# One encoder layer on one core: the mixer's shift and scale in four quarters, each followed by its k/v and q matmuls, and the third group's state update issued behind the gated norm

## The chip, the core and the metric

The kernel runs on one core of a Trainium2 chip. The metric is the device time of one execution in microseconds (us); lower is better. Five engines with queues of their own share the work: TensorE (PE) multiplies, VectorE (DVE), ScalarE (ACT) and GpSimd (POOL) work on tiles in SBUF and PSUM, and SyncE (SP) issues the DMA transfers. Each queue is carried out in order.

## The reference

One layer (DEPTH = 1) of a streaming encoder, for a prompt of 1024 rows and for eight samples of 16 rows, all with model width 1024:

```python
mod = (silu(c) @ w_ada + b_ada)                    # c: one row for the prompt, eight for the samples
sh1, sc1, g1, sh2, sc2, g2 = split(mod, 6)         # each 1024 wide
h = rms_norm(x, norm_mix) * (1 + sc1) + sh1
proj = h @ w_in                                    # z, x/B/C, dt of the SSD heads; q; k and v
y_ssd = ssd_mixer(proj[..., :D_SSD_IN], ...)       # conv, scan in chunks of 64, state update, gated norm
q = rms_norm(q, q_norm); k = rms_norm(k, k_norm)
o = banded_sink_attention(q, k, v, ...)            # window 128, sinks, ALiBi
x = x + g1 * (concat([y_ssd, o]) @ w_out)
h = rms_norm(x, norm_ffn) * (1 + sc2) + sh2
x = x + g2 * ((silu(gate) * up) @ w_down)          # up and gate after a causal conv of width 3
```

The gated norm of the SSD heads is `y = rms_norm(y * silu(z), norm_g)`. The scan also returns its last state, for the prompt and for each of the eight samples.

## The kernel before

**Tiling.** The 1152 rows are three groups g = 0, 1, 2 of 384; the samples are the last 128 rows of g = 2. Activations lie with features on the partitions, in eight feature tiles kt = 0 to 7 of 128. Each fp32 product is three matmuls (`mm3`, L290 to L292): both operands are split in a high part (`wh`, `Rh`) and the rest (`wl`, `Rl`), and high by high, high by low and low by high are added up in PSUM.

**Weights.** `unit` (L74 to L89) loads a unit of 512 KB in one of five buffers `raw` (SP), makes `wh` with a cast on ACT (L80), and `wl` with a subtraction (L86): of q units on POOL, of the others on DVE. There are three buffers of each. For g = 0 each `wl` of the units `kv`, `q`, `f` and `o` is also written to a DRAM tensor `low_*`, and g = 1 and g = 2 read it from there. `W(key)` makes units in the order of `plan` up to two ahead.

**Shift and scale.** The chunks of `w_ada` (512 KB each) pass through the same five `raw` buffers; a chunk is four small matmuls (L156). `ada(c)` adds up eight chunks, copies the sum to `ms` (L174), transposes it (L162) and adds the bias, which gives `mod` (L166); `scale_rows` makes A1 = norm_mix times (1 + sc1) from it (L191). For the mixer this comes in two halves, `ada_half(0)` and `ada_half(1)`, each for four feature tiles of both shift and scale. `mod_steps` then makes, for each feature tile, the scaled row (L251, DVE), the high part `Rh` with the shift (L252, ACT) and the low part `Rl` (L253, DVE). For g = 0 the rows lie in the two tiles `z` (kt 0 to 3) and `qT` (kt 4 to 7).

**The mixer, group by group.** `kv_mm` multiplies k, v and dt (units kv 0 and 1, four feature tiles each), `q_mm` q (units q 0 to 3, two feature tiles each), and `s1_f` the other columns of the projection (ten units f, PSUM tiles named s_f). For g = 0 units kv 0, q 0 and q 1 are multiplied behind the first half and kv 1, q 2 and q 3 behind the second. `attention(g)`, `modulate(g + 1)` and `s1_f(g)` follow. `ssd(g)` is written at the start of the turn of g + 1: for each of three row tiles t, `ssd_1` (decays, masked products; L633 to L666), `ssd_2` (outputs and state; L686 to L723) and `ssd_3` (the gated norm: a sum L752, `rstdy` on DVE L754 and POOL L755, a matmul that spreads it over the partitions L757, then L759 to L761). For g = 2 `ssd_state` (L726 to L743) updates the samples' states: eight multiplies L740 and four adds L742 on tiles of 64x512 and 128x512, and a load and a store each. It is written behind `ssd_3` of the last tile. `out_proj` and then the gated MLP (L987, and `acc` at L1234 to L1240) take the rest.

**What sets the order.** A scheduler places the instructions of all engines by simulated times when the kernel is built; what is ready early in its simulation is placed early, wherever it is written. `tc.issue_after(x)` (used by the change) holds the instructions of a block behind instruction x in that order. On the chip each queue then runs in the order that was laid down.

## Time and profile before

| | us |
|---|---|
| median of three runs | 1321.71 |
| the three runs | 1320.98, 1321.71, 1325.16 |
| the profiled execution, whole time | 1326.11 |
| its span in the trace | 1324.3 |
| granted TensorE clock, mean over the span | 0.976 |

The profile is of one execution, which took 4.4 us longer than the median and 1.8 us longer than its own span. In the rows a line number is a line of the kernel before; `out<-in` names tiles. Starts are microseconds from the start of the span. A bracket at the end of a row is the time for which the engine had been idle, and what released it.

### The profile page before, as it was taken

To read this page: it belongs to the slowest core of one execution; us is meant where nothing else is said; L and a number is where in the kernel's file an instruction comes from. 1 tells how busy PE (TensorE), PEld (TensorE's weight loads), DVE (VectorE), ACT (ScalarE), POOL (GpSimd) and SP (SyncE) were. 2 spreads that over 40 slices of the span, in tenths; PEclk is the share of its full clock that TensorE was granted. 3 is DMA by queue.
4 is the path that set the end of the run, shared out by engine and by line. 5 is a ranking of instruction groups with operands and counts; after the bars stand their busy time and mean duration, and the time that the engine had idled before them with its cause. 6 is when DMAs were issued, how large, how long until landed. Compare 5 with 4: busy or idle time off the path is not lost.

```text
span 1324.3 us, 22453 instructions
## 1 busy us (share of the span) xinstructions
PE 1269.5 (96%) x8545; PEld 1191.4 (90%) x8545; DVE 901.2 (68%) x1793; ACT 626.0 (47%) x1077; POOL 195.6 (15%) x242
## 2 busy tenths in 40 slices
PE   3899989999999899979999999999999999999998
PEld 1688768888878799979999999999999999999998
DVE  4387798566884864796877887766676755654653
ACT  3267736664566425554544445454545433333331
POOL 1131244344310420000011111000000000000000
PEclk8899989999999989989999999999999999999999
DMA  9886524785668469422434434323232897787751
GB/s 346 291 311 214 194 96 173 258 313 218 226 251 287 145 215 358 156 95 85 146 121 139 155 112 130 119 85 121 86 120 73 287 390 239 262 266 221 252 186 51
DMA packets 99948, 257.93 MB, mean 195 GB/s; under 512 B 16544, under 2 KB 47904, under 8 KB 99456
## 3 DMA queue, kind: packets, MB, share of 16 engines
q1 hardware_dynamic: 99840, 256.49, 55.9%
q8 instruction: 67, 1.10, 0.3%
q14 instruction: 41, 0.34, 0.1%
HBM read 202.06 MB, written 54.39 MB: 194 GB/s over the span
## 4 chain that ended last, share of the span: by engine, by line
PE 86%; DVE 9%; DMA 1%; issue 1%; ACT 1%; SPq 0%; POOL 0%; DVEq 0%; ACTq 0%
PE P L987 34%; PE acc L292 7%; PE acc L291 7%; PE acc L290 7%; PE s_f L290 3%; PE s_f L292 3%; PE s_f L291 3%; PE out_proj L290 2%; PE out_proj L292 2%; PE out_proj L291 2%; PE attn_o L532 2%; PE ada L156 2%; PE attn_t L519 1%; PE s_q L292 1%; PE s_q L291 1%
## 5 line engine op out<-in xcount | busy, mean ns | idle before, releaser
L987 PE MATMUL P<-T,wh 128*128 128x288 f32 x704 | 206.5, 296 | 8.2 <-ACT T L915 5.5
L987 PE MATMUL P<-T,wl 128*128 128x288 f32 x704 | 208.1, 296 | 0.0
L80 ACT CAST wh<-raw 128x1024 fp32r<-128x1024 f32 (+1 forms) x138 | 144.8, 1050 | 79.4 <-PE out_proj L292 22.5
L291 PE MATMUL acc<-gh,wl 128*128 128x384 f32 x520 | 174.5, 337 | 0.0
L292 PE MATMUL acc<-gl,wh 128*128 128x384 f32 x520 | 173.0, 337 | 0.3 <-DVE gl L1235 0.3
L290 PE MATMUL acc<-gh,wh 128*128 128x384 f32 x520 | 172.2, 337 | 0.0
L987 PEld LDWEIGHTS P<-T,wh 128*128 128x128 f32 x704 | 132.6, 189 | 8.9 <-ACT T L915 5.7
L987 PEld LDWEIGHTS P<-T,wl 128*128 128x128 f32 x704 | 133.2, 189 | 0.0
L1094 DVE SCALAR_TENSOR_TENSOR uy<-uraw,fw,uy 128x1024 f32<-128x1024 f32 x88 | 112.5, 1279 | 22.6 <-ACT uy L1091 22.5
L86 DVE TENSOR_TENSOR wl<-raw,wh 128x1024 fp32r<-128x1024 f32 (+1 forms) x86 | 107.4, 1248 | 29.2 <-ACT wh L80 29.1
L972 DVE TENSOR_TENSOR wl<-raw,wh 128x512 fp32r<-128x512 f32 x132 | 87.1, 685 | 49.5 <-ACT wh L971 49.5
L1234 ACT CAST gh<-gu 128x384 fp32r<-128x384 f32 x65 | 33.3, 513 | 156.4 <-PE acc L291 142.2
L292 PEld LDWEIGHTS acc<-gl,wh 128*128 128x128 f32 x520 | 98.0, 189 | 0.6 <-DVE gl L1235 0.6
L291 PEld LDWEIGHTS acc<-gh,wl 128*128 128x128 f32 x520 | 97.6, 188 | 0.1
L290 PEld LDWEIGHTS acc<-gh,wh 128*128 128x128 f32 x520 | 97.5, 188 | 0.0
L971 ACT CAST wh<-raw 128x512 fp32r<-128x512 f32 x132 | 76.4, 620 | 31.6 <-PE P L987 30.5
L290 PE MATMUL s_f<-Rh,wh 128*128 128x384 f32 x240 | 83.2, 347 | 0.0
L292 PE MATMUL s_f<-Rl,wh 128*128 128x384 f32 x240 | 82.1, 342 | 0.0
L291 PE MATMUL s_f<-Rh,wl 128*128 128x384 f32 x240 | 81.8, 341 | 0.0
L1124 ACT COPY tm<-P 128x576 f32<-128x576 f32 x48 | 30.5, 635 | 106.5 <-PE P L987 95.2
L1233 DVE TENSOR_TENSOR gu<-gu,gg 128x384 f32<-128x384 f32 x65 | 35.8, 556 | 64.6 <-DMA gu<-gd 51.7
L1096 POOL COPY fso<-uraw 128x2 f32<-128x2 f32 x44 | 11.1, 252 | 447.9 <-DVE uraw L1079 447.9
(357 smaller groups left out, 3424.2 us busy)
## 6 DMA issues: line engine op xcount, KB each, us to landing
raw<-in_w_down SPq DMA_DIRECT2D x66, 512.0 KB, 4.3
raw<-in_w_up SPq DMA_DIRECT2D x50, 512.0 KB, 3.8
gd<-uy SPq DMA_DIRECT2D x44, 576.0 KB, 3.2
raw<-in_w_ada SPq DMA_DIRECT2D x48, 512.0 KB, 6.1
raw<-in_w_f SPq DMA_DIRECT2D x30, 512.0 KB, 5.6
gu<-gd SPq DMA_DIRECT2D x65, 192.0 KB, 3.7
gg<-gd SPq DMA_DIRECT2D x65, 192.0 KB, 3.7
raw<-in_w_out SPq DMA_DIRECT2D x24, 512.0 KB, 4.9
```

Source lines behind the costliest of these rows:

```text
L80: S.copy(wh[:, :n], raw[:, :n])
L86: eng.tensor_tensor(wl[:, :n], raw[:, :n], wh[:, :n].bitcast(F32), op=ALU.subtract)
L290: T.matmul(ps, lh, rh, start=first, stop=False)
L291: T.matmul(ps, ll, rh, start=False, stop=False)
L292: T.matmul(ps, lh, rl, start=False, stop=last)
L971: S.copy(h, x)
L972: V.tensor_tensor(l, x, h.bitcast(F32), op=ALU.subtract)
L987: T.matmul(ps[:, c, 0:HC], x[:, m], y[:, kt, cc], start=first and kt + n == 0, stop=kt == 3 and n == 2, skip_group_check=True)
L1094: V.scalar_tensor_tensor(y[:, :1024], raw[:, j:j + 1024], k[:, j:j + 1], y[:, :1024], op0=ALU.mult, op1=ALU.add)
L1124: S.copy(two(dst), bk(ps))
L1233: V.tensor_tensor(gu, gu, gg, op=ALU.mult)
L1234: S.copy(gh, gu)
```

## The change

The shift and scale of the mixer are made by `ada_quarter(j)` for j = 0 to 3, four chunks of 512 KB each, laid out anew (`w_ad0`) so that a quarter holds shift and scale of feature tiles 2j and 2j + 1; the sum over the model width is now made of two half-sums, added on DVE. Behind each quarter come two feature tiles of `mod_steps`, half a kv unit (18 matmuls) and one q unit (18 matmuls). All k, v and q matmuls of g = 0 are thus written ahead of `s1_kv`.

In `unit`, the low parts of kv and q of g = 0 are made on DVE and not written to DRAM. At g = 1 they are made again, q on POOL and kv on DVE, and written then; g = 2 reads them as before.

For g = 1 each load of a tile `xs` in `mod_steps` is preceded by a copy of one column of A1 into that tile, so that it can't start ahead of the last quarter.

`ssd_state` of g = 2 is put in an `issue_after` block behind the last instruction of `ssd_3`.

```diff
@@ unit
         nm, g, u = k
-        if nm in lows and g > 0:
+        keep = 1 if nm in ("kv", "q") else 0
+        if nm in lows and g > keep:
             nc.sync.dma_start(out=wl[:, :n].bitcast(F32), in_=lows[nm][u])
             return wh, wl
-        eng = G_ if nm in sys_wp else V
+        eng = G_ if nm in sys_wp and g > 0 else V
         eng.tensor_tensor(wl[:, :n], raw[:, :n], wh[:, :n].bitcast(F32), op=ALU.subtract)
-        if nm in lows:
+        if nm in lows and g == keep:
             nc.sync.dma_start(out=lows[nm][u], in_=wl[:, :n].bitcast(F32))
@@ in place of ada
+    def ada_quarter(j):
+        ps = (cps, mps)[j % 2]("ada")
+        for kp in range(4):
+            raw = rawt()
+            nc.sync.dma_start(out=raw[:, :1024], in_=d["w_ad0"][j, kp])
+            for i in range(4):
+                g = 32 * i
+                T.matmul(ps[g:g + 32, :256], cs[:, 2 * kp + i // 2, :], raw[:, i * 256:(i + 1) * 256],
+                         start=kp == 0, stop=kp == 3, tile_position=(0, g))
         ms = ft([P, 256], "ms", 1)
         V.tensor_copy(ms, ps[:, :256])
-        ada_end(c, ms, ps)
+        p2 = ps[:, 256:]
+        for i in range(2):
+            T.transpose(p2[:, i * P:(i + 1) * P], ms[:, i * P:(i + 1) * P], ident)
...
+        V.tensor_tensor(m, v[:, 0:2], b.unsqueeze(3).broadcast_to([P, 2, 2, 9]), op=ALU.add)
+        V.tensor_tensor(m, m, v[:, 2:4], op=ALU.add)
+        f = slice(2 * j, 2 * j + 2)
+        V.scalar_tensor_tensor(A1[:, f, :], mod[:, 8 + 2 * j:10 + 2 * j, :], 1.0,
+                               C["nm"][:, f].unsqueeze(2).broadcast_to([P, 2, 9]), op0=ALU.add, op1=ALU.mult)
@@ mod_steps
                 xs = ft([P, GN], "xs", 3)
+                if g == 1:
+                    V.tensor_copy(xs[:, 0:1], A1[:, 7, 0:1])
                 nc.sync.dma_start(out=xs, in_=src[:, kt, :])
@@ kv_mm
-    def kv_mm(g, h, ps, us, ws=None):
+    def kv_mm(g, h, ps, us, ws=None, ks=range(4)):
@@ ssd
         if g == 2:
-            ssd_state(one[2] + (hBs,))
+            with tc.issue_after(traced()):
+                ssd_state(one[2] + (hBs,))
@@ the start
-    ada_half(0)
-    ws = [W(k, 0) for k in (("kv", 0, 0), ("q", 0, 0), ("q", 0, 1))]
+    ada_quarter(0)
...
+    for j in range(4):
+        if j % 2 == 0:
+            kvw = W(("kv", 0, j // 2), 0)
+        qw = W(("q", 0, j), 0)
+        for _ in range(2):
+            next(steps, None)
+        if j < 3:
+            ada_quarter(j + 1)
+        kv_mm(0, h, kvps, [j // 2], kvw, (2 * (j % 2), 2 * (j % 2) + 1))
+        q_mm(0, h, qps, [j], qw)
```

On SyncE, the loads at the start of the kernel. Before, behind `cs`, `xT` and `cst`:

```order
L153 DMA raw<-in_w_ada 128x1024 x5
L237 DMA xs<-in_xT 128x384 x3
L153 DMA raw<-in_w_ada 128x1024 x3
L77 DMA raw<-in_w_kv 128x1056
L77 DMA raw<-in_w_q 128x1024 x2
L153 DMA raw<-in_w_ada 128x1024 x2
L88 DMA low_kv<-wl 128x1056
L153 DMA raw<-in_w_ada 128x1024
L88 DMA low_q<-wl 128x1024
L153 DMA raw<-in_w_ada 128x1024 x2
L88 DMA low_q<-wl 128x1024
L153 DMA raw<-in_w_ada 128x1024 x3
```

After, behind the same loads:

```order
L174 DMA raw<-in_w_ad 128x1024 x4
L77 DMA raw<-in_w_kv 128x1056
L77 DMA raw<-in_w_q 128x1024
L174 DMA raw<-in_w_ad 128x1024 x4
L77 DMA raw<-in_w_q 128x1024
L174 DMA raw<-in_w_ad 128x1024 x4
L77 DMA raw<-in_w_kv 128x1056
L77 DMA raw<-in_w_q 128x1024
L174 DMA raw<-in_w_ad 128x1024 x4
L77 DMA raw<-in_w_q 128x1024
L291 DMA raw<-in_xk 128x1024 x3
L77 DMA raw<-in_w_f 128x1024 x4
```

The weights of k, v and q now stand between the quarters' chunks, the writes of `low_kv` and `low_q` are gone from here, and the first loads of `xs` and of the units f stand behind all of it.

On VectorE, `ssd(0)` at its gated norm of the first row tile, while the weights of g = 1 are made. Before (`rstdy` is the norm's factor, `wl` a weight's low part, `sz` the state):

```order
L715 TENSOR_TENSOR sz<-sz,ssd_st 64x256 x2
L86 TENSOR_TENSOR wl<-raw,wh 128x1024
L754 TENSOR_SCALAR rstdy<-ssd_n 128x1
L750 TENSOR_REDUCE ys<-qn 128x128
L759 SCALAR_TENSOR_TENSOR z<-z,cst,ssd_n 128x128 x4
```

After:

```order
L733 TENSOR_TENSOR sz<-sz,ssd_st 64x256 x2
L772 TENSOR_SCALAR rstdy<-ssd_n 128x1
L87 TENSOR_TENSOR wl<-raw,wh 128x1024
L768 TENSOR_REDUCE ys<-qn 128x128
L777 SCALAR_TENSOR_TENSOR z<-z,cst,ssd_n 128x128 x4
```

The factor `rstdy` (L754 before, L772 after) has passed one making of a low part.

On VectorE, `ssd(2)` from the sum of the first row tile's norm to its factor. Before (`qT` holds the samples' states, `P` their decays):

```order
L750 TENSOR_REDUCE ys<-qn 128x128
L652 TENSOR_SCALAR PT<-ssd_rp,acs 128x128 x4
L740 TENSOR_TENSOR qT<-qT,P 64x512 x4
L714 TENSOR_TENSOR sz<-sz,P 64x256
L656 TENSOR_TENSOR PT<-PT,GT 128x512
L665 TENSOR_TENSOR xdt<-ssd_px,dt 128x512
L714 TENSOR_TENSOR sz<-sz,P 64x256
L719 SCALAR_TENSOR_TENSOR xbc<-xbc,cst,ssd_y 128x128 x4
L740 TENSOR_TENSOR qT<-qT,P 64x512 x2
L656 TENSOR_TENSOR PT<-PT,GT 128x512
L715 TENSOR_TENSOR sz<-sz,ssd_st 64x256
L754 TENSOR_SCALAR rstdy<-ssd_n 128x1
```

After, from the same sum:

```order
L768 TENSOR_REDUCE ys<-qn 128x128
L670 TENSOR_SCALAR PT<-ssd_rp,acs 128x128 x4
L732 TENSOR_TENSOR sz<-sz,P 64x256
L674 TENSOR_TENSOR PT<-PT,GT 128x512
L683 TENSOR_TENSOR xdt<-ssd_px,dt 128x512
L732 TENSOR_TENSOR sz<-sz,P 64x256
L737 SCALAR_TENSOR_TENSOR xbc<-xbc,cst,ssd_y 128x128 x4
L674 TENSOR_TENSOR PT<-PT,GT 128x512
L733 TENSOR_TENSOR sz<-sz,ssd_st 64x256 x2
L772 TENSOR_SCALAR rstdy<-ssd_n 128x1
```

The six state multiplies (L740 before, L758 after) are gone from ahead of `rstdy`; they now stand behind the last instruction of the third tile's gated norm (L779), and one small instruction on `sz` has come ahead of `rstdy`.

## Rows read from the trace of the kernel before

**Rows 1.** The page: busy time of PE; its busy tenths in 40 slices.

```profile
PE 1269.5 (96%) x8545; PEld 1191.4 (90%) x8545; DVE 901.2 (68%) x1793; ACT 626.0 (47%) x1077; POOL 195.6 (15%) x242
...
PE   3899989999999899979999999999999999999998
```

**Rows 2.** Three stretches: length, busy us of each engine, clock, DMA share, GB/s.

```profile
20.00:40.00 20.00, 12.77 (x79) 7.63 (x80) 10.41 (x13) 5.74 (x8) 4.65 (x2) 0.66 0.96 362
...
180.00:200.00 20.00, 14.60 (x74) 12.22 (x73) 17.63 (x38) 6.60 (x11) 6.15 (x6) 0.66 0.30 105
...
460.00:480.00 20.00, 16.36 (x82) 15.80 (x83) 17.28 (x34) 3.91 (x7) 7.46 (x7) 0.66 0.63 218
```

**Rows 3.** PE in time, the start: start, duration, line, operation, [idle before].

```profile
14.27 5.35 PE L156 MATMUL ada<-raw,cs 128*32 128x256 f32 x48 [0.30 <-issue]
...
22.90 1.08 PE L156 MATMUL ada<-raw,cs 128*32 128x256 f32 x8 [1.49 <-DMA raw<-in_w_ada]
...
32.34 1.03 PE L290 MATMUL s_kv<-wh,Rh 128*128 128x264 f32 x3 [3.24 <-ACT Rh L252]
...
54.63 0.62 PE L290 MATMUL s_kv<-wh,Rh 128*128 128x264 f32 x3 [1.92 <-ACT Rh L252]
...
72.50 0.59 PE L290 MATMUL s_f<-Rh,wh 128*128 128x384 f32 x2
```

**Rows 4.** PE in time, pairs of successive matmuls at the start of the kernel.

```profile
46.00 0.39 PE L291 MATMUL s_q<-wh,Rl 128*128 128x512 f32 x1
46.23 0.40 PE L292 MATMUL s_q<-wl,Rh 128*128 128x512 f32 x1
...
61.40 0.63 PE L290 MATMUL s_q<-wh,Rh 128*128 128x512 f32 x1
61.83 0.63 PE L291 MATMUL s_q<-wh,Rl 128*128 128x512 f32 x1
...
64.13 0.28 PE L292 MATMUL s_kv<-wl,Rh 128*128 128x264 f32 x1
64.25 0.29 PE L290 MATMUL s_kv<-wh,Rh 128*128 128x264 f32 x1
```

**Rows 5.** DVE in time, the two scale steps of the start.

```profile
26.63 2.35 DVE L191 SCALAR_TENSOR_TENSOR A<-mod,cst 128x36 f32<-128x36 f32 x1
29.09 4.14 DVE L251 SCALAR_TENSOR_TENSOR z<-z,A,rs 128x384 f32<-128x384 f32 x4
...
53.08 0.20 DVE L191 SCALAR_TENSOR_TENSOR A<-mod,cst 128x36 f32<-128x36 f32 x1
```

**Rows 6.** POOL in time, two low parts of q weights.

```profile
26.57 4.65 POOL L86 TENSOR_TENSOR wl<-raw,wh 128x1024 fp32r<-128x1024 f32 x2 [11.47 <-ACT wh L80]
```

**Rows 7.** DVE in time, `ssd(0)` ahead of the first gated norm.

```profile
184.58 1.61 DVE L86 TENSOR_TENSOR wl<-raw,wh 128x1024 fp32r<-128x1024 f32 x1
```

**Rows 8.** PE's waits: line waited for, us in total, times, longest.

```profile
PE ssd_n L757 <- POOL rstdy L755: 10.0, 3, 5.5
```

**Rows 9.** DVE in time, `ssd(2)`: the state multiplies and the factor.

```profile
453.54 2.77 DVE L740 TENSOR_TENSOR qT<-qT,P 64x512 f32<-64x512 f32 x4
...
459.49 2.35 DVE L740 TENSOR_TENSOR qT<-qT,P 64x512 f32<-64x512 f32 x2
...
462.81 0.14 DVE L754 TENSOR_SCALAR rstdy<-ssd_n 128x1 f32<-128x1 f32 x1
```

**Rows 10.** PE in time, the same stretch and the matmuls behind it.

```profile
457.24 0.28 PE L752 MATMUL ssd_n<-cst,ys 128*128 128x1 f32 x2
...
463.64 0.79 PE L757 MATMUL ssd_n<-cst,rstdy 128*128 128x128 f32 x2 [5.49 <-POOL rstdy L755]
...
476.25 0.48 PE L292 MATMUL out_proj<-Rl,wh 128*128 128x384 f32 x1
476.57 0.34 PE L290 MATMUL out_proj<-Rh,wh 128*128 128x384 f32 x1
476.75 0.34 PE L291 MATMUL out_proj<-Rh,wl 128*128 128x384 f32 x1
```

More of the change, by code (lines that the diff above doesn't have):

```diff
@@ L152, in ada_mm @@
             raw = rawt()
-            nc.sync.dma_start(out=raw[:, :1024], in_=d["w_ada"][c, kt])
+            nc.sync.dma_start(out=raw[:, :1024], in_=d["w_ada"][c - 2, kt])
             for i in range(4):
@@ L163, in ada_end @@
         v = p2.rearrange("p (i g r) -> p g i r", i=2, g=4)[:, :, :, 0:9]
-        for f0, a, b in ((4 * c, 0, 2), (8 + 4 * c, 2, 4)) if c < 2 else ((8 * c, 0, 4),):
-            f1 = f0 + 2 * (b - a)
-            V.tensor_tensor(mod[:, f0:f1, :].rearrange("p (g i) r -> p g i r", i=2), v[:, a:b],
-                            C["bada"][:, f0:f1].rearrange("p (g i) -> p g i", i=2).unsqueeze(3)
-                            .broadcast_to([P, b - a, 2, 9]), op=ALU.add)
-    def ada(c, bank):
-        ps = bank("ada")
-        ada_mm(ps, c, 0, 8)
+        f0 = 8 * c
+        V.tensor_tensor(mod[:, f0:f0 + 8, :].rearrange("p (g i) r -> p g i r", i=2), v,
+                        C["bada"][:, f0:f0 + 8].rearrange("p (g i) -> p g i", i=2).unsqueeze(3)
+                        .broadcast_to([P, 4, 2, 9]), op=ALU.add)
+    def ada_quarter(j):
[7 more added lines that the diff above has]
+                         start=kp == 0, stop=kp == 3, tile_position=(0, g))
         ms = ft([P, 256], "ms", 1)
         V.tensor_copy(ms, ps[:, :256])
-        ada_end(c, ms, ps)
+        p2 = ps[:, 256:]
+        for i in range(2):
+            T.transpose(p2[:, i * P:(i + 1) * P], ms[:, i * P:(i + 1) * P], ident)
+        v = p2.rearrange("p (i g r) -> p g i r", i=2, g=4)[:, :, :, 0:9]
+        m = mod[:, 0:16, :].rearrange("p (s j i) r -> p s j i r", s=2, j=4)[:, :, j]
+        b = C["bada"][:, 0:16].rearrange("p (s j i) -> p s j i", s=2, j=4)[:, :, j]
+        V.tensor_tensor(m, v[:, 0:2], b.unsqueeze(3).broadcast_to([P, 2, 2, 9]), op=ALU.add)
[3 more added lines that the diff above has]
+                               C["nm"][:, f].unsqueeze(2).broadcast_to([P, 2, 9]), op0=ALU.add, op1=ALU.mult)
     def ada_part(i):
@@ L315, in kv_mm @@
             for t in range(3):
-                for k in range(4):
+                for k in ks:
                     kt = 4 * u + k
@@ L806, in out_proj @@
         rstd_of(ss, 1024, rstd2[:, g, :])
-    def ada_half(half):
-        ada(half, (mps, cps)[half])
-        scale_rows(A1, C["nm"], 2, half)
     x0 = [ft([P, 4, GN], tag) for tag in ("z", "qT")]
@@ L821, in body @@
     r = s0_stats(0, x0)
-    ada_half(0)
-    ws = [W(k, 0) for k in (("kv", 0, 0), ("q", 0, 0), ("q", 0, 1))]
+    ada_quarter(0)
     h = [R(), R()]
     kvps = [gps("s1_kv") for _ in range(3)]
+    qps = [cps("s1_q") for _ in range(3)]
     steps = mod_steps(0, x0, r, A1, 0, h)
-    for kt in steps:
-        if kt == 3:
-            break
     next(steps)
-    ada_half(1)
-    qps = [cps("s1_q") for _ in range(3)]
-    kv_mm(0, h, kvps, [0], ws[0])
-    q_mm(0, h, qps, [0], ws[1])
-    q_mm(0, h, qps, [1], ws[2])
-    for kt in steps:
-        pass
+    for j in range(4):
[8 more added lines that the diff above has]
+        q_mm(0, h, qps, [j], qw)
     hs = {0: h}
@@ L859, in body @@
             mixS[g - 1] = ssd(g - 1, *dat[g - 1])
[L860 to L862 removed]
+        if g > 0:
             kvps = [gps("s1_kv") for _ in range(3)]
@@ L1295 @@
     A["cT"] = cT
-    wa = I["w_ada"][0].reshape(8, P, 12, 512)[:, :, [0, 2, 1, 3] + list(range(4, 12))]
-    A["w_ada"] = cc(wa.reshape(8, P, 6, 1024).transpose(2, 0, 1, 3))
+    wa = I["w_ada"][0]
+    A["w_ad0"] = cc(wa[:, :2048].reshape(4, 2, P, 2, 4, 256).transpose(4, 0, 2, 1, 3, 5).reshape(4, 4, P, 1024))
+    A["w_ada"] = cc(wa[:, 2048:].reshape(8, P, 4, 1024).transpose(2, 0, 1, 3))
     wi = I["w_in"][0]
```

7 lines of the change are left out of this document (1 added, 6 removed).

## The prediction

> **What bounds the kernel now.** I read first the page: TensorE is busy for 1269.5 of 1324.3 us, and of the 40 slices of the span only a few hold less than nine tenths [rows 1]. So a change can win only where TensorE stands still or runs at the lower of its two clocks (2.4 and 1.2 GHz). Next I read the stretches, to find where that is: 20 to 40 us has 12.77 busy of 20 at a mean granted clock of 0.66, 180 to 200 us 14.60 at 0.66, 460 to 480 us 16.36 at 0.66 [rows 2]. The change touches all three, so each was read in TensorE's order of time.
>
> In the start the reader is to see waits for an ada sum and what is made from it: 1.49 us for a chunk, 3.24 us until the first k/v matmul at 32.34, and 1.92 us behind the second half at 54.63; the first matmul of s_f comes at 72.50 [rows 3]. The three slices behind it, 66 to 165 us, show nines [rows 1], so an earlier 72.50 should move what follows with it. In `ssd(0)` and `ssd(2)` TensorE waits for the factor of the gated norm, 10.0 us in three waits, the longest 5.5 [rows 8].
>
> **Part 1, the quarters.** *What a quarter costs.* Successive q matmuls start 0.23 us apart at the full clock and 0.43 at the low one; k/v matmuls 0.12 at the full clock [rows 4]; at the low one I take twice that, 0.24 or a little less. A quarter has 18 of each: 18 x 0.12 + 18 x 0.23 = 6.3 us at the full clock, about 11.8 at the low one. Four ada chunks cost 4 x 1.08 = 4.3 at the low clock [rows 3] and, halved, 2.2 at the full one; two transposes, by the k/v matmuls the nearest in width, stay under 0.5. That is 9.0 us a quarter, and with about 0.4 for handing on the rows 9.4. Its loads are four chunks, a q unit and half a kv unit, 2.9 MB; at the 362 GB/s of 20 to 40 us [rows 2] 8.0 us, just under TensorE's 9.4.
>
> *When the first begins.* Six chunks are done 5.35 us after 14.27 [rows 3], so four by about 17.9. In the old start the end of the eight chunks (22.90 + 1.08 = 23.98) and the first k/v matmul lie 8.4 us apart. Of this the step for A took 2.35 us where the same step took 0.20 in the second half, and the four steps on z 4.14 [rows 5], while POOL was making low parts of q, 4.65 us from 26.57 [rows 6]. The change puts these on VectorE, at most 1.61 us each by the one seen there [rows 7]; A comes in quarters of the size, with an add more (about 0.2, the duration of the unhindered A). I take 3.6 us in place of 8.4 and get 17.9 + 3.6 = 21.5.
>
> The Trainium skill, "SBUF — State Buffer", section "SBUF: two separate sides", says that VectorE with two inputs in SBUF and a GpSimd instruction that reads SBUF share a port pair as an exclusive lock, and the later one waits in full. The long A and the long first step on z agree with it; by that rule the start gains and `ssd(0)`, below, pays.
>
> *The sum of the start.* The first quarter runs in part at the low clock, and its q unit waits for one of five raw buffers: 13.0 us to the start of the second (9.4, some 2.5 for five us at half the rate, 1.1 for the load). The third begins 9.3 later, the fourth 9.0 later, and its own matmuls, with a cast of an f unit ahead of its `Rh` on ACT, take 6.6: 21.5 + 13.0 + 9.3 + 9.0 + 6.6 = 59.4. Against 72.5 this is **13 us gained**; 8 if each quarter waits some 1.7 us more (as behind the second half, 1.92 [rows 3]), 15 if the first warms up sooner.
>
> *Taken at nothing.* The six writes of low parts leave the start and come back at g = 1 in place of six loads of the same size, under full TensorE work and little DMA (105 GB/s in 180 to 200 us [rows 2]). Eight copies of a column cost some 0.16 us each on VectorE, by the smallest of the rows, 0.14 [rows 9]: 1.3 us, under the matmuls of s_f; without that cover it would be 1.3 on the path.
>
> **Part 2, ssd(0).** The low parts of q are now made on POOL at g = 1, four of 4.65 / 2 = 2.3 us [rows 6], between the products of `ssd(0)`. Where VectorE runs an instruction with two tiles beside one, it may stretch up to that length: from 0 to 4 x 2.4 = 9.6 us, in a stretch where it is near its limit (17.63 of 20 [rows 2]). On the other side `rstdy` stood behind a low part of 1.61 us [rows 7], now ahead of it, and four more q matmuls (0.9 us) stand where TensorE waited. I take a **gain of 2**, bounds a loss of 9 and a gain of 5: two of the four stand on POOL ahead of the work that VectorE hurries with, and the two kv low parts that VectorE gets come early.
>
> **Part 3, ssd(2).** The sum of the first tile's norm is ready at 457.5, but the factor comes on VectorE only at 462.81, behind six state multiplies of 2.77 and 2.35 us [rows 9]; TensorE stands still for 5.49 us and then runs at the low clock up to 476.25: out_proj matmuls come 0.32 us apart there and 0.17 to 0.18 behind it [rows 10]. With the six gone (5.12) and one state add put ahead (half the columns of a multiply of 2.77 / 4, some 0.4), the factor comes some 4.4 us earlier, and TensorE's wait shrinks to about 1.1. If the clock stays up after so short a wait, the 12.6 us from 463.64 to 476.25 take half, 6.3 less. That is 10.7; I take **10** since the first tile's outputs behind the factor must also be ready sooner than they had to be. The bounds: 4.4 if the clock falls all the same, 12 if the other two norms gain as well.
>
> *What is queued behind.* The six multiplies and three adds now stand behind the last gated norm in one row, about 7 us of VectorE; behind them wait the evictions of out_proj. Three PSUM banks of 24 matmuls (24 x 0.175 = 4.2 us each) cover 8.4, so I take it at nothing; without that cover it costs up to 3. POOL's two masks and the four store issues on SP move with it, and nobody but the end of the kernel waits for the stores.
>
> **Sum.** 13 + 2 + 10 = 25 us. Against the profiled execution 1326.1 - 25 = 1301.1; that execution was 4.4 above the median of the runs, so **1297** against 1321.7.
>
> **The rivals.**
> *The clock falls in ssd(2) all the same*, since a wait of one us remains and others may follow in the small products: part 3 gives 4.5, the whole 1302. For it speaks that the small products wait for VectorE and POOL often; against it, that TensorE is fully busy ahead of it.
> *POOL in the way at g = 1.* All four low parts stretch VectorE in full: part 2 loses 9.6 where I have a gain of 2, and 1297 becomes 1308. For it speak rows 5 and 6, where two out of two did that; against it, that much of that VectorE work reads PSUM and has only one tile in SBUF.
> *The loads hold the quarters.* At 362 GB/s a quarter's loads need 8.0 of its 9.4 us; five buffers may be too few to keep that rate, since a load begins only when a buffer is free. With 2 to 3 us more in each of three quarters part 1 gives 5: 1305.
> *Slower: the quarters never warm up.* If TensorE stops ahead of each quarter and the clock is low through all four, a quarter costs 11.8 + 4.3 + 0.7 and a wait of 1.9, near 18.7, and the first s_f comes at 21.5 + 3 x 18.7 + 11.8 = 89.4, 17 later than before. With part 3 then at 4.5 and part 2 at nothing the whole is 12 slower, 1334; with part 3 whole it is 7 slower. The point from which it decides: with parts 2 and 3 paying 12, a quarter's turn over 17 us in place of 9.4. For it speaks that after each ada wait in the old start the clock was low (0.66 in 20 to 40 us); against it, that the next quarter's ada matmuls stand inside each quarter, and that the old interleaved matmuls at 46 us ran 0.23 apart. The Trainium skill, "TensorE: Matmul & The Clock Gate", section "HAM oscillation — how this bites in real kernels", describes just this: little compute between waits for loads, each time at the cold clock; it would make this case the likely one. The pair at 46 us, between ada chunks, does not agree with it.
> *The change doesn't do what it says.* In the third part the order on VectorE is plain, so only the size is in doubt; in the first, the interleaving might leave the old waits in other places, which is the case of the loads.
>
> **How the numbers follow.** My forecast has a chance of 0.52 (1292 to 1301). The fallen clock has 0.14 (1302), POOL in the way 0.13 (1303 to 1309), the loads 0.11 (1305, up to 1312 with a second mishap), the cold quarters 0.04, and a gain over 30 us 0.06. The range 1289 to 1309 leaves out the cold quarters, the far end of the loads and of POOL, and part of the large gain, about 0.15. A measurement of this kernel can tell about 0.3%, 4 us: all cases but the cold quarters and two mishaps at once lie more than that below 1321.7, so faster 0.92, same 0.04, slower 0.04.
>
> **What would show it.** In the profile after: the first s_f matmul near 59; a first k/v matmul near 21.5; the scale steps of the start at 0.2 and 0.6 us each; four quarters some 9 us apart at a granted clock near 1 from the second on. In `ssd(2)`, a wait for `rstdy` of about 1 us and out_proj matmuls 0.175 apart right behind the small products. The forecast is wrong if s_f begins after 64, if out_proj still comes 0.32 apart there, or if the wait for `rstdy` in `ssd(0)` grows beyond 3.2 us.

## The result: 0.7% faster, where 2% was forecast, and the profile after

| | kernel before | changed kernel |
|---|---|---|
| median, us | 1324.30 (9 runs, 1320.98 to 1325.98) | 1314.01 (9 runs, 1312.58 to 1319.35) |
| ratio, 95% interval | 1 | 0.9931, 0.9915 to 0.9947 |
| profiled execution, its span, us | 1326.11, 1324.3 | 1312.58, 1310.5 |
| mean granted clock of the span | 0.976 | 0.986 |

The changed kernel is 10.3 us faster by the medians (their ratio is 0.9922; the ratio in the table goes by all the runs). The forecast was 1297, with a range of 1289 to 1309: the sign is right, the size is not, and 1314 lies above the range. The profiled execution of before took longer than any of the nine timed runs of its kernel and that of the changed kernel was the fastest of its nine, so the two traces lie 13.5 us apart and the kernels only 10.3. Below, a single trace is used to see where something happens, and medians to say what it is worth.

The page of the changed kernel, the rows that answer to [rows 1]:

```profile
PE 1262.9 (96%) x8549; PEld 1186.5 (91%) x8549; DVE 903.9 (69%) x1815; ACT 626.0 (48%) x1077; POOL 193.5 (15%) x242
...
PE   5899889999999999979999999999999999999998
```

The stretches of [rows 2], and one between them (length, busy us of PE, PEld, DVE, ACT, POOL, granted clock, DMA share, GB/s):

```profile
20.00:40.00 20.00, 16.09 (x110) 10.21 (x110) 10.30 (x22) 4.41 (x6) 0.00 (x0) 0.83 0.82 287
...
140.00:160.00 20.00, 17.59 (x115) 13.99 (x114) 16.15 (x37) 12.71 (x32) 9.48 (x7) 1.00 0.30 103
...
180.00:200.00 20.00, 13.78 (x75) 12.04 (x74) 17.34 (x40) 6.23 (x10) 8.09 (x7) 0.74 0.30 106
...
460.00:480.00 20.00, 20.00 (x115) 20.00 (x115) 14.30 (x27) 7.24 (x11) 8.93 (x9) 0.91 0.95 317
```

The first and the last of the three stretches of [rows 2] have become better (12.77 to 16.09 busy us, 16.36 to 20.00). The middle one has not (14.60 to 13.78), and 140 to 160 us, where TensorE had been busy throughout, now has a hole of 2.4 us. That is the first sign of what went wrong (the work in a stretch of the same times is not quite the same, since it now comes some us earlier).

TensorE in time, the start (answers to [rows 3]):

```profile
22.63 1.03 PE L308 MATMUL s_kv<-wh,Rh 128*128 128x264 f32 x3 [1.89 <-ACT Rh L270]
...
36.66 0.63 PE L308 MATMUL s_kv<-wh,Rh 128*128 128x264 f32 x3 [0.60 <-ACT Rh L270]
...
56.99 0.63 PE L308 MATMUL s_kv<-wh,Rh 128*128 128x264 f32 x3 [2.83 <-ACT Rh L270]
...
65.57 0.42 PE L308 MATMUL s_f<-Rh,wh 128*128 128x384 f32 x1
```

The first s_f matmul comes at 65.57 us in place of 72.50: 6.9 us gained, not 13. TensorE in time at the gated norm of `ssd(0)` and of `ssd(2)` (the latter answers to [rows 10]):

```profile
185.43 0.79 PE L775 MATMUL ssd_n<-cst,rstdy 128*128 128x128 f32 x2 [3.31 <-POOL rstdy L773]
```

```profile
456.61 0.49 PE L775 MATMUL ssd_n<-cst,rstdy 128*128 128x128 f32 x2 [0.89 <-POOL rstdy L773]
457.03 1.09 PE L704 MATMUL ssd_y<-PT,xdt 128*64 128x128 f32 x16
458.05 1.97 PE L717 MATMUL ssd_y<-cz,PT 128*128 128x32 f32 x16
```

TensorE in time before, behind the wait of 5.49 in [rows 10]:

```profile
464.37 1.98 PE L686 MATMUL ssd_y<-PT,xdt 128*64 128x128 f32 x16
466.27 3.62 PE L699 MATMUL ssd_y<-cz,PT 128*128 128x32 f32 x16
```

In `ssd(2)` the gated norm went as forecast: the wait is 0.89 where it was 5.49, and the small products behind it take half the time. Only the out_proj matmuls behind those still stand 0.32 us apart for a while (461.94 to 464.97). In `ssd(0)` the matmul that spreads the factor comes at 185.43 where it came at 187.06 in the trace before. Of the 6.9 us at the first s_f, 1.6 are left here.

So one number tells the two halves of the question apart, and it is given for each run below: **the way**, from the first s_f matmul to that first spread of `rstdy` in `ssd(0)`. It was 187.06 - 72.50 = 114.6 us before and is 185.43 - 65.57 = 119.9 us now. All of `s_f(0)`, the shift and scale of g = 1, its k, v and q matmuls and most of `ssd(0)` lie on it. TensorE's work on it is the same in every run, 737 to 739 matmuls that keep it busy for 111.3 to 113.8 us, so the way measures mostly how much TensorE is held up. The stretch of the way before, in the changed kernel and in e7 (a run below), as in [rows 2]:

```profile
72.50:187.06 114.56, 111.38 (x738) 93.15 (x738) 96.33 (x224) 73.97 (x155) 41.60 (x40) 1.00 0.58 206
65.57:185.43 119.86, 112.37 (x739) 93.62 (x738) 102.49 (x239) 76.15 (x162) 49.67 (x44) 1.00 0.55 190
62.84:176.75 113.91, 111.29 (x738) 92.85 (x736) 94.92 (x237) 76.65 (x162) 42.47 (x40) 1.00 0.61 213
```

TensorE stands still for 3.2 us of it before, 7.5 in the changed kernel and 2.6 in e7. VectorE is busy for 96.3, 102.5 and 94.9 us.

### The profile page after: what moved, and what is told of

The parts are those of the page before. It is cut to its first block, busy times and chain, and to the rows that moved or that the text cites. A ratio compares the mean times of both kernels' runs of the same rounds, so it can differ in the third digit from the quotient of the medians.

```text
span 1310.5 us, 22477 instructions
## 1 busy us (share of the span) xinstructions
PE 1262.9 (96%) x8549; PEld 1186.5 (91%) x8549; DVE 903.9 (69%) x1815; ACT 626.0 (48%) x1077; POOL 193.5 (15%) x242
## 4 chain that ended last, share of the span: by engine, by line
PE 83%; DVE 11%; ACT 2%; issue 2%; DMA 2%; POOL 0%; DVEq 0%; SPq 0%; ACTq 0%
PE P L998 34%; PE acc L310 7%; PE acc L309 7%; PE acc L308 7%; PE s_f L308 3%; PE s_f L309 3%; PE s_f L310 3%; PE out_proj L308 2%; PE out_proj L310 2%; PE out_proj L309 2%; PE attn_o L550 1%; PE ada L157 1%; PE s_q L309 1%; PE s_q L310 1%; DVE PT L670 1%
## 5 line engine op out<-in xcount | busy, mean ns | idle before, releaser
L87 DVE TENSOR_TENSOR wl<-raw,wh 128x1024 fp32r<-128x1024 f32 (+1 forms) x92 | 113.9, 1238 | 23.4 <-ACT wh L80 23.2
```

Source lines behind the costliest of these rows:

```text
L87: eng.tensor_tensor(wl[:, :n], raw[:, :n], wh[:, :n].bitcast(F32), op=ALU.subtract)
```

## The experiments

Twelve kernels were run, each beside runs of the kernel before on the same chip. The table has the ratio to the kernel before with its 95% interval, and from each run's trace the first s_f matmul, the first spread in `ssd(0)` and the way between them. Medians of different rows come from different runs of the kernel before (1322.5 to 1324.3), so differences of 1 to 2 us between rows tell nothing.

| run | median, us | ratio (interval) | first s_f | spread | way |
|---|---|---|---|---|---|
| before | 1322.5 to 1324.3 | 1 | 72.50 | 187.06 | 114.6 |
| changed | 1314.01 | 0.9931 (0.9915 to 0.9947) | 65.57 | 185.43 | 119.9 |
| e1 changed without the state update's move | 1320.84 | 0.9991 (0.9978 to 1.0004) | 62.82 | 183.22 | 120.4 |
| e2 before with the state update's move alone | 1314.13 | 0.9935 (0.9920 to 0.9951) | 71.78 | 186.34 | 114.6 |
| e3 q low parts of g = 1 on VectorE | 1315.22 | 0.9942 (0.9929 to 0.9954) | 64.97 | 185.85 | 120.9 |
| e4 xs loads not held back | 1316.28 | 0.9942 (0.9928 to 0.9955) | 64.99 | 183.40 | 118.4 |
| e5 low parts at g = 0, written on SyncE | 1308.19 | 0.9887 (0.9865 to 0.9908) | 62.95 | 180.84 | 117.9 |
| e6 statistics of g = 1 later | 1312.61 | 0.9919 (0.9905 to 0.9934) | 61.09 | 181.83 | 120.7 |
| e7 low parts at g = 0, written on POOL's queue | **1305.02** | **0.9859** (0.9842 to 0.9875) | 62.84 | 176.75 | 113.9 |
| e8 e6 and e7 together | 1312.13 | 0.9917 (0.9903 to 0.9932) | 63.08 | 183.48 | 120.4 |
| e9 e2 with the low parts at g = 1, halves | 1319.86 | 0.9972 (0.9959 to 0.9985) | 67.42 | 189.47 | 122.1 |
| e10 e7 with halves in place of quarters | 1312.49 | 0.9925 (0.9908 to 0.9941) | 68.06 | 183.20 | 115.1 |
| e11 e7 without holding the xs loads | 1310.09 | 0.9906 (0.9885 to 0.9926) | 62.29 | 178.34 | 116.1 |
| e12 e7 with kv's low parts at g = 1 | 1309.45 | 0.9899 (0.9871 to 0.9926) | 63.93 | 180.77 | 116.8 |

### Which part brought the gain: e1 and e2

e1 takes the state update's move out of the changed kernel, e2 puts it alone into the kernel before:

```diff
         if g == 2:
-            with tc.issue_after(traced()):
-                ssd_state(one[2] + (hBs,))
+            ssd_state(one[2] + (hBs,))
```

```diff
         if g == 2:
-            ssd_state(one[2] + (hBs,))
+            with tc.issue_after(traced()):
+                ssd_state(one[2] + (hBs,))
```

> The changed kernel with the state update of the third group back in its old place (the quarters, the low parts at g = 1 and the held xs loads stay). Theory: in the changed kernel's trace the last part gains some 11 us, the start 7 us at the first s_f, and about 5 us of those are lost again between 128 and 185 us; so this run is 2 to 3 us faster than the kernel before (ratio 0.998), with the wait for rstdy in ssd(2) near 5.5 us and out_proj matmuls 0.32 us apart behind it. Rival: the quarters carry most of the gain and the last part little; then this run is 7 us or more faster than before (0.995 or less).

> The kernel before with nothing changed but the state update of the third group queued behind the gated norm. Theory: 9 to 11 us faster than before (ratio 0.992 to 0.993), wait for rstdy in ssd(2) about 1 us; the rest of the trace as before. Rival (the quarters carry the gain): 3 us or less faster.

e1 is 0.9991, with 1 in its interval; e2 is 0.9935, just short of its theory's 0.992 to 0.993. The move of the state update alone is worth as much as the whole change, and the rest of the change nothing that can be told apart from zero (the interval runs from 2.9 us faster to 0.5 slower). TensorE in time at the gated norm of `ssd(2)`, first e1, then e2:

```profile
458.14 0.80 PE L775 MATMUL ssd_n<-cst,rstdy 128*128 128x128 f32 x2 [5.52 <-POOL rstdy L773]
458.86 1.98 PE L704 MATMUL ssd_y<-PT,xdt 128*64 128x128 f32 x16
```

```profile
457.91 0.49 PE L757 MATMUL ssd_n<-cst,rstdy 128*128 128x128 f32 x2 [0.91 <-POOL rstdy L755]
458.33 1.09 PE L686 MATMUL ssd_y<-PT,xdt 128*64 128x128 f32 x16
```

The wait of 5.52 and the doubled duration are there exactly where the move is not. Yet in e1's trace the first s_f comes at 62.82, 9.7 us earlier than before. The theory was right that this is given back; that it is given back on the way, 120.4 against 114.6 us, the table shows.

### What gives it back: e3, e4, e5 and e7

The trace of the changed kernel between 130 and 190 us shows three things. First VectorE and POOL in time, from one view each:

```profile
133.53 2.13 DVE L269 SCALAR_TENSOR_TENSOR xs<-xs,A,rs 128x384 f32<-128x384 f32 x1 [2.07 <-DMA xs<-in_xT]
...
144.30 2.72 DVE L267 TENSOR_TENSOR Rl<-xs,Rh 128x384 fp32r<-128x384 f32 x1
...
168.13 3.22 DVE L393 SCALAR_TENSOR_TENSOR sp_p<-sp_p,sp_s 128x24 f32<-128x24 f32 x4
```

```profile
132.85 2.39 POOL L87 TENSOR_TENSOR wl<-raw,wh 128x1024 fp32r<-128x1024 f32 x1
...
143.91 2.69 POOL L87 TENSOR_TENSOR wl<-raw,wh 128x1024 fp32r<-128x1024 f32 x1
...
156.44 2.71 POOL L87 TENSOR_TENSOR wl<-raw,wh 128x1024 fp32r<-128x1024 f32 x1
...
168.19 2.35 POOL L87 TENSOR_TENSOR wl<-raw,wh 128x1024 fp32r<-128x1024 f32 x1
...
183.82 1.55 POOL L773 TENSOR_TENSOR rstdy<-rstdy,cst 128x1 f32<-128x1 f32 x1
```

Three of POOL's four subtractions lie beside a long VectorE row that outlasts them by 0.4 us in the first two and by 0.8 in the last: 2.72 us for a step that takes 0.55 in e3's trace, 3.22 for four steps on 24 elements. Beside the one at 156.44 VectorE works on tiles in PSUM (four steps in 1.11 us from 156.82, no longer than elsewhere). In the last row it is the other way round: POOL's power of one column takes 1.55 us, while VectorE makes a low part from 183.74 on; it took 0.55 to 0.56 at 186.46 and 463.03 in the trace before. TensorE in time and SyncE in time there:

```profile
136.76 0.63 PE L308 MATMUL s_kv<-wh,Rh 128*128 128x264 f32 x3 [0.62 <-ACT Rh L266]
...
139.40 0.39 PE L309 MATMUL s_kv<-wh,Rl 128*128 128x264 f32 x1 [0.84 <-DVE xs L254]
...
143.23 1.06 PE L537 MATMUL attn_t<-cst,P 128*128 128x128 f32 x8 [1.73 <-DVE P L528]
...
147.07 0.39 PE L309 MATMUL s_kv<-wh,Rl 128*128 128x264 f32 x1 [0.68 <-DVE Rl L267]
```

```profile
126.96 0.33 SPq L89 DMA_DIRECT2D low_kv<-wl  x1
127.39 0.37 SPq L255 DMA_DIRECT2D xs<-in_xT  x1
```

TensorE stops four times, 3.9 us in all, for the shift and scale of g = 1 and for the attention beside it. And the load of the fourth xs tile stands on SyncE behind the write of a low part that VectorE made only at 125.69 to 126.93, where before a low part was read and none written; the copy that holds this load ends on VectorE at the same time (126.85 to 126.99). Three suspects, then: POOL beside VectorE, the additional work as such, and the late xs loads. The edits:

```diff
@@ e3
-        eng = G_ if nm in sys_wp and g > 0 else V
+        eng = V
@@ e4
-                if g == 1:
-                    V.tensor_copy(xs[:, 0:1], A1[:, 7, 0:1])
@@ e5
-        keep = 1 if nm in ("kv", "q") else 0
+        keep = 0
-        eng = G_ if nm in sys_wp and g > 0 else V
+        eng = V
@@ e7: e5, and
-            nc.sync.dma_start(out=lows[nm][u], in_=wl[:, :n].bitcast(F32))
+            (nc.gpsimd if nm in ("kv", "q") else nc.sync).dma_start(out=lows[nm][u], in_=wl[:, :n].bitcast(F32))
```

> The changed kernel with the low parts of the q weights at g = 1 made on VectorE in place of POOL. Theory (POOL's work beside VectorE stretches the shift and scale of g = 1 and TensorE waits for it): no VectorE step of that shift and scale over 1.5 us (2.13 and 2.72 us before), the four TensorE waits of together 3.9 us between 136 and 148 us down to 1 or less, whole time 2 to 4 us less than the changed kernel. Rival (the loads of xs come late there, or VectorE has too much work in ssd(0)): waits as they are, or moved to rstdy in ssd(0), time the same or up to 4 us more.

e3 did what it should to the steps (0.55 to 0.62 us each in the shift and scale of g = 1 behind 133 us), and nothing for the time: 1315.22, way 120.9. The waits moved to `rstdy`, as its rival had it. The largest of TensorE's waits between 100 and 200 us in e3 (line waited for, us in total, times, longest):

```profile
PE ssd_n L775 <- POOL rstdy L773: 6.2, 2, 4.5
```

So POOL's place beside VectorE is not the cause by itself: four subtractions of 1.2 to 2.0 us on VectorE (130.30 to 166.05), which is busy for 19.72 of 20 us between 160 and 180, cost as much as four of 2.35 to 2.71 us on POOL.

> The changed kernel without the copies that hold back the xs loads of g = 1. Theory: the late loads of xs at g = 1 stand behind the writes of low_kv on SyncE and behind their three buffers, not behind the copies, so the waits between 136 and 148 us stay; in the start three loads of 192 KB come early and cost up to 2 us. Whole time the same or up to 2 us more. Rival (the copies make the loads late): the waits at 136 to 148 us go, 2 to 4 us less.

e4's waits for the shift and scale of g = 1 did shrink, to one of 0.8 us, which speaks for the rival; but the way is still 118.4, `rstdy` is waited for 3.5 us at its end, and the whole time is 1316.28, not 2 to 4 us less than the changed kernel's. So neither expectation held in full: the copies have a part in the waits, and taking them away gains nothing. That the start would lose up to 2 us didn't show at the first s_f (64.99).

> The changed kernel with the low parts of kv and q made and written at g = 0 as before (on VectorE, the writes on SyncE between the loads of the start); g = 1 and g = 2 read them. Theory: the six subtractions at g = 1 (four of 2.3 to 2.7 us on POOL that stretch VectorE, two of 1.2 on VectorE) are what gives the start's gain back; without them the way from the first s_f to the first spread of the gated norm in ssd(0) is 115 us or less (119.9 in the changed kernel, 114.6 before). The writes make the first s_f 1 to 5 us later than 65.6. Whole time 0 to 4 us less than the changed kernel. Rival (the stretch from s_f to ssd(0) is bound by VectorE and ScalarE whatever is done to the weights): the way stays at 118 to 120 us and the whole time gets worse by what the start loses.

> As the run with the low parts at g = 0, but the six writes issued on POOL's queue, so that SyncE's loads don't stand behind them. Theory: first s_f within 1 us of the changed kernel's 65.6, way from there to the first spread in ssd(0) 115 us or less, whole time 3 to 5 us less than the changed kernel. Rival (bound by VectorE and ScalarE anyway): way 118 to 120 us, time as the changed kernel's within 1 us.

With the subtractions back at g = 0 the time falls to 1308.19 (e5) and, with the writes off SyncE, to 1305.02 (e7): 9.0 us below the changed kernel, more than the 3 to 5 of e7's theory. The intervals of e5 and e7 overlap, so what the writes' queue is worth isn't settled. e7's way is 113.9; e5's is 117.9, and its theory's 115 or less did not come. The largest of TensorE's waits between 100 and 200 us in e7:

```profile
PE ssd_n L775 <- POOL rstdy L773: 4.0, 2, 2.1
```

Of the waits for the shift and scale of g = 1 one of 0.5 us is left. e5's start was expected to be 1 to 5 us later than the changed kernel's, e7's within 1 us of it; they were 2.6 and 2.7 us earlier (62.95, 62.84). Some of that may be chance: the stretch 20 to 40 us has a clock of 0.83 in the changed kernel, e6 and e7, and 1.00 in e1, e3, e4 and e5, while e1's engines have the same order there as the changed kernel's.

### Are the quarters worth anything: e9 and e10

e9 puts the low parts at g = 1 into e2, which has halves; e10 puts e7's way of making and writing them into e2. The edits are those of the change's `unit`, and of e7, on e2; neither has the copies that hold back the xs loads.

> The kernel before (halves, not quarters) with the state update queued behind the gated norm and the low parts of kv and q made and written at g = 1 as in the changed kernel. Theory: the way from the first s_f to the first spread of the gated norm in ssd(0) grows from 114.6 us to 117 to 120, as in the changed kernel, although no quarter is there; the start itself gains 1 to 4 us since POOL no longer stands in VectorE's way there. Whole time within 3 us of the run with the state update alone (1314.1), and not below 1310. Rival (the way is long because the quarters bring everything closer together): the way stays at 115 us and the whole time is 2 to 4 us less than 1314.

> The kernel before with the state update queued behind the gated norm, the low parts of kv and q made on VectorE at g = 0 and written on POOL's queue: what the fast version has, but with halves. Theory: the first s_f comes 2 to 4 us earlier than 71.8 (A and the first scale step on z and qT no longer stretched), the way from there to ssd(0) stays at 114 to 115 us, whole time 2 to 4 us less than 1314.1, so that the quarters are worth 5 to 7 of the 9 us between 1314 and 1305. Rival (it is the queue of the writes and the place of the subtractions, not the quarters): 1305 to 1308.

e9: way 122.1, the longest of all, with halves. This refutes the rival (that the quarters bring things together too closely): the low parts at g = 1 lengthen the way with halves as with quarters. The whole time is 5.8 us above e2's, more than the theory's 3. The largest of TensorE's waits between 100 and 200 us in e9 shows where:

```profile
PE ssd_n L758 <- POOL rstdy L756: 10.7, 2, 7.4
```

The start of e9 did gain (67.42 against e2's 71.78), and VectorE's step for A takes 0.19 there in place of 2.35 [rows 5].

e10 has the short way (115.1), and halves: 1312.49, 1.6 us less than e2 where 2 to 4 were expected. With this the four corners are there:

| | low parts at g = 1 | low parts at g = 0, written on POOL's queue |
|---|---|---|
| halves | e9 1319.9 | e10 1312.5 |
| quarters | changed 1314.0 | e7 1305.0 |

All four have the state update's move. The low parts at g = 1 cost 7.4 us in the one row and 9.0 in the other. The lower row is 5.9 us faster in the one column and 7.5 in the other, but it differs from the upper one in two things, the quarters and the held xs loads. Quarters without the held loads are e4 (1316.3) and e11 (1310.1, below): 3.6 and 2.4 us faster than the halves. So the quarters alone are worth 2 to 4 us and the held loads 2 to 5, each good to some 2 us. Against e2 (1314.1), the changed kernel gained some 6 by the two together and lost as much to the low parts.

### What in the low parts: e11 and e12

e11 is e7 without the copies that hold back the xs loads (e4's edit on e7). e12 is e7 with the low parts of kv, not of q, at g = 1:

```diff
-        keep = 0
+        keep = 1 if nm == "kv" else 0
...
-            (nc.gpsimd if nm in ("kv", "q") else nc.sync).dma_start(out=lows[nm][u], in_=wl[:, :n].bitcast(F32))
+            (nc.gpsimd if nm == "q" else nc.sync).dma_start(out=lows[nm][u], in_=wl[:, :n].bitcast(F32))
```

> The version with the low parts at g = 0 written on POOL's queue, without the copies that hold back the xs loads of g = 1. Theory: those loads of 0.6 MB then run in the start among the chunks (loads of 346 GB/s there, so some 1.7 us), first s_f 1 to 2 us later than 62.8, whole time 0 to 3 us more than 1305. Rival (the copies cost VectorE more than they save): 1 to 2 us less.

> The fast version (low parts at g = 0, written on POOL's queue), but with those of kv alone made at g = 1 on VectorE and written there on SyncE, as in the changed kernel; q stays at g = 0. Theory: of the 9 us between the fast version and the changed kernel the four q subtractions of 2.3 to 2.7 us on POOL carry most and the two kv ones of 1.2 us on VectorE 1 to 3: whole time 1306 to 1308, way from the first s_f to the first spread in ssd(0) 115 to 117 us. Rival (the writes of low_kv, behind which the loads of xs stand on SyncE, are the cause): 1311 or more, with TensorE's waits of 3 to 4 us between 130 and 148 us back.

e11 is 5 us slower than e7: the held loads are worth it, more than was thought, though its first s_f is no later (62.29); the loss lies on the way and behind it, and isn't followed further here. e12 is 4.4 us slower than e7 by the medians, though the intervals just touch. Its way of 116.8 is within its theory, but its time is neither the theory's (1306 to 1308) nor the rival's (1311 or more): the two kv subtractions and their writes carry about half of the 9 us, which would leave the four q ones the other half if the two simply add up. TensorE in time in e12:

```profile
138.25 0.62 PE L308 MATMUL s_kv<-wh,Rh 128*128 128x264 f32 x3 [2.75 <-ACT Rh L266]
```

That is the wait for the shift and scale of g = 1. VectorE and SyncE in time in e12, up to the load of its fourth to sixth xs tile:

```profile
124.28 1.24 DVE L87 TENSOR_TENSOR wl<-raw,wh 128x1056 fp32r<-128x1056 f32 x1
...
127.72 0.14 DVE L254 COPY xs<-A 128x1 f32<-128x1 f32 x1
```

```profile
125.55 0.33 SPq L89 DMA_DIRECT2D low_kv<-wl  x1
...
127.92 1.44 SPq L255 DMA_DIRECT2D xs<-in_xT  x3
```

The xs load is issued at 127.92 where it is issued at 122.44 in e7. What released it is not the write of `low_kv`, which had gone out at 125.55, but the copy that holds it, at 127.72 on VectorE; in e7 the copy stands at 122.28. Ahead of the copy VectorE makes the kv low part at 124.28. So in this trace the load is late because VectorE comes late to the copy, and the rival's cause, the write on SyncE, isn't shown. How the price is shared between the subtractions, their writes and POOL's stretching stays open, since e3 traded the one for the other without a gain and e12 moved kv's subtractions and writes together.

### The start: e6 and e8

The last quarter's wait of 2.83 us in the changed kernel has a row of its own on VectorE and on ScalarE. VectorE in time, then ScalarE in time:

```profile
53.04 0.18 DVE L190 SCALAR_TENSOR_TENSOR A<-mod,cst 128x18 f32<-128x18 f32 x1
55.30 0.17 DVE L294 TENSOR_SCALAR rstd<-ss 128x3 f32<-128x3 f32 x1 [2.08 <-ACT raw L292]
55.37 1.14 DVE L269 SCALAR_TENSOR_TENSOR qT<-qT,A,rs 128x384 f32<-128x384 f32 x2
```

```profile
54.12 1.06 ACT L292 ACTIVATE raw<-raw 128x1024 f32<-128x1024 f32 x1 [0.30 <-PE s_q L309]
...
55.37 1.04 ACT L80 CAST wh<-raw 128x1024 fp32r<-128x1024 f32 x1
56.32 1.12 ACT L270 ACTIVATE Rh<-qT,mod 128x384 fp32r<-128x384 f32 x2
```

The row statistics of g = 1, which nothing needs before 120 us, stand ahead of the last quarter's scale step on both engines, and the cast of an f unit ahead of its `Rh`. A is ready at 53.2, `Rh` begins at 56.32. Then the clock falls. A stretch of the last quarter:

```profile
59.00:61.00 2.00, 2.00 (x10) 1.90 (x10) 0.15 (x2) 0.00 (x0) 0.00 (x0) 0.51 1.02 323
```

e6 queues both behind the last quarter's own steps (`issue_after` holds the instructions of one engine only, so two are nested):

```diff
-            hs[1] = modulate(1, d["xT"][1], s0_stats(1), A1, 0)
+            with tc.issue_after(last["Rh"]), tc.issue_after(last["Rl"]):
+                r1 = s0_stats(1)
+            hs[1] = modulate(1, d["xT"][1], r1, A1, 0)
...
+        if k == ("f", 0, 0):
+            with tc.issue_after(last["Rh"]):
+                S.copy(wh[:, :n], raw[:, :n])
...
```

What is left out here keeps the cast of the other units as it was and notes the last `Rh` and `Rl` of g = 0 in `last`.

> The changed kernel with the row statistics of g = 1 and the cast of the first f unit queued behind the last quarter's high and low parts on ScalarE and VectorE. Theory: the wait of 2.83 us ahead of the last quarter falls to 1.5 or less and the first s_f comes 1.5 to 4 us earlier (62 to 64 us); most of that is given back by the way from s_f to ssd(0), so the whole time is 0 to 2 us less. Rival (the start's gain arrives in full): 2 to 4 us less.

> The two before together: low parts at g = 0 written on POOL's queue, statistics of g = 1 and first f cast behind the last quarter. Theory: first s_f at 62 to 64 us, way to the first spread in ssd(0) 115 us or less, whole time 4 to 8 us less than the changed kernel (ratio to before 0.987 to 0.990). Rival: way 118 us or more, time within 2 us of the changed kernel.

TensorE in time in e6, the last quarter:

```profile
54.62 0.64 PE L318 MATMUL s_kv<-wh,Rh 128*128 128x264 f32 x3 [0.41 <-ACT Rh L276]
```

The wait fell from 2.83 to 0.41 and the quarter's matmuls from 8.6 to 6.5 us: 4.5 us at the first s_f (61.09). The whole time fell by 1.4 (1312.61), the way is 120.7: given back, as the theory had it. e8 was to have both gains and has neither: 1312.13. Its first s_f is at 63.08, but the scheduler laid `ssd(0)` down in another order, with three low parts of w_out ahead of the factor where e7 has one (172.57, with the factor at 175.00). VectorE in time in e8, and TensorE's wait there:

```profile
159.98 1.23 DVE L93 TENSOR_TENSOR wl<-raw,wh 128x1024 fp32r<-128x1024 f32 x1 [0.76 <-ACT wh L87]
...
167.58 2.27 DVE L93 TENSOR_TENSOR wl<-raw,wh 128x1024 fp32r<-128x1024 f32 x1
...
176.39 1.23 DVE L93 TENSOR_TENSOR wl<-raw,wh 128x1024 fp32r<-128x1024 f32 x1 [0.24 <-ACT wh L87]
...
181.82 0.14 DVE L782 TENSOR_SCALAR rstdy<-ssd_n 128x1 f32<-128x1 f32 x1
```

```profile
183.48 0.80 PE L785 MATMUL ssd_n<-cst,rstdy 128*128 128x128 f32 x2 [6.42 <-POOL rstdy L783]
```

This is the same place and the same kind of work as in the changed kernel, brought there by an edit 110 us earlier. e8 thus has a way of 120.4 with no kv or q low part made at g = 1: an edit of the start, through the order that came of it, cost 7 us (1312.13 against 1305.02). That leaves a rival to the reading of the four corners, whose orders differ too. Between 165 us and the factor, one low part of w_out stands on VectorE in the changed kernel (172.85) and in e7 (172.57), and two in e9 (169.37, 176.59) and in e10 (169.89, 180.93). So within a row of that table this part of the order is the same, and it doesn't explain the 7.4 and 9.0 us between the columns; it may have a share in what lies between the rows. How much else of the order the scheduler changed with each edit, and what that is worth, no run here separates. Why e8's order came out so wasn't looked into.

## Why the prediction was wrong, point by point

**The bound.** The step that failed is "so an earlier 72.50 should move what follows with it", together with the two terms that the prediction put on the way: the low parts at g = 1 as a part of a gain of 2 in `ssd(0)`, and their writes at nothing. It was argued from slices in which TensorE is nine tenths busy. That holds only as long as the other engines deliver as much earlier, and on the way they didn't once they had more to do: the way grew from 114.6 to 119.9 us with the same matmuls on it, and VectorE's busy time there from 96.3 to 102.5. (That busy time doesn't decide alone: e5's is 95.8, with a way of 117.9.) Where the low parts stayed at g = 0 (e7), the gain of the start did arrive in full: 8.9 us at the first s_f against e2, 9.6 at the first spread, 9.1 in the median. All three signs by which the prediction said it would be wrong came: s_f after 64 (65.57), out_proj matmuls 0.32 apart (462.41 and 462.73), and a wait for `rstdy` in `ssd(0)` over 3.2 us (3.31).

**Part 1, the quarters.** The mechanism was right, the size too large. At the first s_f 13 was forecast, and the traces with this start and no further edit to it show 65.57 and 62.82, 6.9 and 9.7 earlier. Of the sum, the first quarter's start was 22.63 in place of 21.5; the second's 36.66 in place of 34.5; the fourth's 56.99 in place of 52.8; and its matmuls took 8.6 in place of 6.6. The largest single miss is the last two, and e6 measured it: 4.5 us, the statistics of g = 1 and a cast in front, with the clock that falls behind the wait. The cast was seen and priced; the statistics on VectorE, and the clock, were not. The 13 also holds what the start gains when POOL no longer makes low parts there, which e9 shows without quarters (71.78 to 67.42). In the whole time the quarters are worth 5.9 (changed against e9) to 7.5 us (e7 against e10) with the held xs loads, and 2.4 to 3.6 without them; the copies that hold the loads were priced as a cost alone.

**"Taken at nothing".** The six writes in place of six loads at g = 1 were taken at nothing because TensorE was busy and the DMA queues were not. Not looked at was that a write needs the low part to be made first, and that the xs loads come behind work on VectorE. e12 prices kv's subtractions and writes together at 4.4 us; the writes alone have no price in these runs.

**Part 2, ssd(0).** A gain of 2 was taken; the low parts at g = 1 cost 7.4 to 9.0. The bounds had a loss of 9, so the range held it, but it was given a chance of 0.13 as the rival "POOL in the way". That rival named the right part and about the right size, but not a mechanism that holds by itself: the long steps are in the trace (2.13, 2.72, 3.22 us beside POOL's rows), but e3 removed them and nothing was gained. The reason given against the rival, that much of VectorE's work there reads PSUM, fits the subtraction at 156.44, but missed that the shift and scale of g = 1, which reads two tiles of SBUF, lies on the way too. `rstdy` did pass the low part, as the order showed, and the low part behind it then slowed POOL's power from 0.55 to 1.55 us, which is 1.0 of the wait of 3.31.

The Trainium skill, "SBUF — State Buffer", section "SBUF: two separate sides", has VectorE with two SBUF inputs and a GpSimd instruction that reads SBUF lock each other out, whichever is first. The rows agree in both directions; what the rule does not tell is whether the lock or the work is the price, and here e3 says that moving the work to VectorE was no cure.

**Part 3, ssd(2).** Right but for its last piece. A gain of 10 was forecast; e2 measured 8.8 us by the medians (1322.96 to 1314.13). In the changed kernel's trace the wait fell by 4.6 us (5.49 to 0.89), where 4.4 had been worked out (5.12 less 0.4 is 4.7), and the small products by 4.2 (1.98, 3.62 and 3.60 to 1.09, 1.97 and 1.95). Out_proj behind them ran at the lower clock for as long as before in the changed kernel (461.94 to 464.97; before, 473.55 to 476.25), and not in e2, whose stretch from 460 to 480 us has a clock of 1.00. The queue behind it, taken at nothing, cost nothing that the trace shows: the state multiplies now stand at 484.10 to 488.31 and from 498.57, and TensorE is busy all the while:

```profile
480.00:500.00 20.00, 20.00 (x107) 18.09 (x106) 10.46 (x20) 6.69 (x10) 2.87 (x3) 1.00 0.89 314
```

**The other rivals.** The quarters that never warm up did not happen: from 36.6 to 54.1 us the clock is 1.00, and TensorE, with the next quarter's chunks set among the matmuls of each, is at work for 16.12 of 17.50 us there. The Trainium skill, "TensorE: Matmul & The Clock Gate", section "HAM oscillation — how this bites in real kernels", tells of little compute between waits for loads, with the low clock again behind each wait. Here the longest wait for a chunk behind the first, 1.32 us at 39.53, was not followed by it; the wait of 2.83 us for ScalarE was (0.51 over 59 to 61 us). The loads that hold the quarters: that wait of 1.32 us is smaller than the rival's 2 to 3 us a quarter.

**The sum as it came out**, one step after the other by the medians: state update -9 (before to e2; -10 forecast), low parts at g = 1 with what the start gains by them +6 (e2 to e9), quarters -4 (e9 to e4), held xs loads -2 (e4 to the changed kernel). The forecast had -13 for all that happens in the start and -2 for `ssd(0)`. Together it comes to -9, and -10 was measured; each part is good to some 2 us, so the last one can't be told from nothing.

**A better version** is e7: the changed kernel with the low parts of kv and q made on VectorE at g = 0 and written there on POOL's queue. It takes 1305.02 us, 0.9859 of the kernel before and 9 us less than the changed kernel.

## What to carry to other kernels

An engine that is busy nearly all the time is the bound only while the others keep up; before an earlier start is counted as a gain of the whole, look in each later stretch for the engine that is second, and at what the change adds to it. Work that is moved to where TensorE is busy anyway must be priced on the engines that do it: six subtractions and six writes, taken as a small gain or as nothing, cost 7 to 9 us. When a change has several parts, run each alone: here one part carried the whole gain, and the others cancelled. And where a scheduler lays down the order, an edit in one place can change the order in another; look at it before the difference is put down to the edit.
